# Rotary embedding of 67 MB: casts in the DMA queue against fp32 transfers with casts on ScalarE

## The chip, the cores and the metric

The kernel runs on one core of a Trainium2 chip. The metric is device time in microseconds (us) for one launch. The time before is 323.0 us, the median of 10 runs, which lie between 322.83 and 323.29 us. The profile is one execution taken by the hardware profiler; its time span starts with the program's first instructions and ends with its last.

## The reference

The input x has the shape (8, 2048, 16, 64): batch, position, head, and 64 values per head, all fp32. The 64 values are 32 neighbouring pairs. Each pair is turned by an angle that depends on the position and on the pair's number, given as tables of cosines and sines of the shape (2048, 32):

```python
x1 = x_pairs[..., 0]
x2 = x_pairs[..., 1]
out1 = x1 * cos - x2 * sin
out2 = x1 * sin + x2 * cos
out = np.stack([out1, out2], axis=-1).reshape(batch, seq_len, num_heads, head_dim)
```

x has 67.1 MB and so has the output; the two tables have 0.26 MB each. Each value of x is used for two products, so there is little arithmetic for each byte moved.

## The kernel before

A tile is 512 positions of one batch: 128 partitions, each with 4 consecutive positions (K = 4) of 16 heads of 64 values, which is 4,096 values per partition. In memory a tile is one contiguous block of 2.1 MB, 16 KiB for each partition. There are 4 groups of positions (the loop over g) and 8 batches (the loop over b inside it), together 32 tiles.

The kernel computes in bf16. The load of a tile (L73) is issued by GpSimd and converts from fp32 to bf16 on the way; the store (L86) is issued by GpSimd too and converts back. No engine does a cast of x. Both use one software DMA queue, in the order in which GpSimd issues them.

Ahead of the loops SP issues eight small loads that bring the tables, group by group, into cos_sb and sin_sb (L50, L51). For each group ScalarE expands them (build_tables, L53 to L64): for each of the 4 positions, one copy writes the cosine twice for each pair and once for every head (L61), and two write the sine and the negated sine in turn (L62, L63). The results c_tab and s_tab have 4,096 values per partition, as large as a tile of x. This makes 48 ScalarE instructions.

For each tile VectorE runs three operations. The first multiplies x by the sine table into qt (L78), the second x by the cosine table into pt (L79), and the third adds to pt the values of qt with the two of each pair exchanged (L84). The exchange costs no instruction: it is an access pattern that starts at the second value and steps back by one.

There are 5 buffers for x, 4 for qt, 4 for pt, and 3 for each expanded table. A buffer's next user waits until the last reader of it is done. The order of instructions on an engine is not written out by hand: the framework's scheduler orders them, and it lets VectorE work on the operations of two neighbouring tiles in turn. GpSimd's queue holds loads and stores; a store waits there for its addition, and a load for a free x buffer.

Of the kernel before, what the change touches and what calls it, by code (L numbers as in the profile page):

```python
# [2 lines left out]

# [4 lines left out]


@with_exitstack  # L10
def kernel(
    ctx: ExitStack,
    tc: tile.TileContext,
    x: bass.AP,
    cos: bass.AP,
    sin: bass.AP,
    out: bass.AP,
):
    nc = tc.nc
    fp32 = mybir.dt.float32  # L20
    bf16 = mybir.dt.bfloat16
    mult = mybir.AluOpType.mult
    add = mybir.AluOpType.add

    B, S, H, D = x.shape
    P = 128
    K = 4
    G = S // (P * K)
    D2 = D // 2
    HD = H * D  # L30
    W = K * HD
    ntiles = B * G

    TAIL_SPLIT = 0

    x_t = x.rearrange("b (g p k) h d -> (b g) p (k h d)", p=P, k=K)
    out_t = out.rearrange("b (g p k) h d -> (b g) p (k h d)", p=P, k=K)
    cos_g = cos.rearrange("(g p k) c -> g p (k c)", p=P, k=K)
    sin_g = sin.rearrange("(g p k) c -> g p (k c)", p=P, k=K)

    consts = ctx.enter_context(tc.tile_pool(name="consts", bufs=1))
    tabpool = ctx.enter_context(tc.tile_pool(name="tabpool", bufs=3))
    xpool = ctx.enter_context(tc.tile_pool(name="xpool", bufs=5))
    qpool = ctx.enter_context(tc.tile_pool(name="qpool", bufs=4))
    opool = ctx.enter_context(tc.tile_pool(name="opool", bufs=4))

    cos_sb = consts.tile([P, G, K, D2], fp32)
    sin_sb = consts.tile([P, G, K, D2], fp32)
    for g in range(G):
        nc.sync.dma_start(out=cos_sb[:, g], in_=cos_g[g])  # L50
        nc.sync.dma_start(out=sin_sb[:, g], in_=sin_g[g])  # L51

    def build_tables(g):  # L53
        c_tab = tabpool.tile([P, W], bf16, name="c_tab")
        s_tab = tabpool.tile([P, W], bf16, name="s_tab")
        c_dst = c_tab.rearrange("p (k h i j) -> p k h i j", k=K, h=H, i=D2, j=2)
        s_dst = s_tab.rearrange("p (k h i j) -> p k h i j", k=K, h=H, i=D2, j=2)
        for k in range(K):
            c_src = cos_sb[:, g, k : k + 1, :].to_broadcast([P, H, D2, 2])
            s_src = sin_sb[:, g, k : k + 1, :].to_broadcast([P, H, D2])  # L60
            nc.scalar.copy(out=c_dst[:, k], in_=c_src)  # L61
            nc.scalar.copy(out=s_dst[:, k, :, :, 0], in_=s_src)  # L62
            nc.scalar.mul(out=s_dst[:, k, :, :, 1], in_=s_src, mul=-1.0)  # L63
        return c_tab, s_tab  # L64

    tile_idx = 0
    for g in range(G):
        c_tab, s_tab = build_tables(g)
        for b in range(B):
            i = b * G + g  # L70

            xt = xpool.tile([P, W], bf16)
            nc.gpsimd.dma_start(out=xt, in_=x_t[i])  # L73

            qt = qpool.tile([P, W], bf16)
            pt = opool.tile([P, W], bf16)

            nc.vector.tensor_tensor(out=qt, in0=xt, in1=s_tab, op=mult)  # L78
            nc.vector.tensor_tensor(out=pt, in0=xt, in1=c_tab, op=mult)  # L79
            q_swap = dataclasses.replace(  # L80
                qt, offset=qt.offset + 1, ap=[qt.ap[0], [2, W // 2], [-1, 2]]
            )
            pt3 = pt.rearrange("p (a j) -> p a j", a=W // 2, j=2)
            nc.vector.tensor_tensor(out=pt3, in0=pt3, in1=q_swap, op=add)  # L84

            nc.gpsimd.dma_start(out=out_t[i], in_=pt)  # L86
            tile_idx += 1


# [1 line left out]
_INS = ['x', 'cos', 'sin']  # L91
_OUTS = [((8, 2048, 16, 64), 'float32')]


# [23 lines left out]
```

## Time and profile before

| What | Value |
|---|---|
| Median of 10 runs | 323.0 us |
| The profiled execution | 322.89 us |
| Its span | 321.1 us |
| VectorE busy | 213.2 us (66%), 96 operations |
| ScalarE busy | 36.8 us (11%), 48 table instructions and one table load |
| GpSimd busy | 34.5 us (11%), 64 DMA issues and 4 memsets |
| Read from and written to HBM | 67.63 MB and 67.11 MB, 420 GB/s over the span |
| Median time from issue to landing | load of x 22.7 us, store 12.6 us |

The profile divides the span into 40 equal slices of 8.03 us. A digit is the busy share of an engine in a slice, in tenths; the DMA row is the mean busy share of the core's 16 DMA engines, and GB/s is what they moved, counted on the side that is written. A row of a group of instructions gives the line, the engine, the operation, the output and the inputs with their sizes, then the count, the total busy time in us and the mean duration of one in ns, and after the second bar the idle time of the engine just ahead of these instructions and what ended most of it. A DMA share above 1 in a stretch comes from packets that overlap on one DMA engine.

### The profile page before, as it was taken

To read this page: it belongs to the slowest core of one execution; us is meant where nothing else is said; L and a number is where in the kernel's file an instruction comes from. 1 tells how busy PE (TensorE), PEld (TensorE's weight loads), DVE (VectorE), ACT (ScalarE), POOL (GpSimd) and SP (SyncE) were. 2 spreads that over 40 slices of the span, in tenths; PEclk is the share of its full clock that TensorE was granted. 3 is DMA by queue.
4 is the path that set the end of the run, shared out by engine and by line. 5 is a ranking of instruction groups with operands and counts; after the bars stand their busy time and mean duration, and the time that the engine had idled before them with its cause. 6 is when DMAs were issued, how large, how long until landed. Compare 5 with 4: busy or idle time off the path is not lost.

```text
span 321.1 us, 304 instructions
## 1 busy us (share of the span) xinstructions
DVE 213.2 (66%) x96; ACT 36.8 (11%) x49; POOL 34.5 (11%) x68
## 2 busy tenths in 40 slices
DVE  0799887601999900999910999920899920899930
ACT  8698100000820000000000000000000000000000
POOL 3010100400010030010030001030001030001000
DMA  7999999999999999999999999999999999999994
GB/s 138 217 218 216 346 329 431 429 433 244 214 215 398 431 437 251 216 213 385 436 431 266 214 214 376 431 431 281 215 216 359 431 433 294 215 214 346 435 435 176
DMA packets 10370, 101.21 MB, mean 315 GB/s; under 512 B 1152, under 2 KB 2176, under 8 KB 2176
## 3 DMA queue, kind: packets, MB, share of 16 engines
q0 software_dynamic: 9216, 100.67, 101.6%
q1 hardware_dynamic: 1152, 0.52, 1.1%
q14 instruction: 2, 0.02, 0.0%
HBM read 67.63 MB, written 67.11 MB: 420 GB/s over the span
## 4 chain that ended last, share of the span: by engine, by line
DVE 42%; DMA 35%; issue 15%; POOL 3%; POOLq 0%; DVEq 0%; PEldq 0%
DMA xt<-in_x_dram 28%; DVE pt L84 17%; DVE qt L78 13%; DVE pt L79 13%; DMA out_dram<-pt 7%; POOL xt L73 2%; POOL out_dram L86 1%; POOLq L113 0%; POOLq L86 0%; DVEq L78 0%; PEldq L113 0%
## 5 line engine op out<-in xcount | busy, mean ns | idle before, releaser
L78 DVE TENSOR_TENSOR qt<-xt,s_tab 128x4096 bf16<-128x4096 bf16 x32 | 73.2, 2289 | 79.9 <-DMA xt<-in_x_dram 79.8
L79 DVE TENSOR_TENSOR pt<-xt,c_tab 128x4096 bf16<-128x4096 bf16 x32 | 73.2, 2288 | 14.3 <-ACT c_tab L61 10.1
L84 DVE TENSOR_TENSOR pt<-pt,qt 128x4096 bf16<-128x4096 bf16 x32 | 73.2, 2288 | 0.2
L86 POOL DMA_DIRECT2D out_dram<-pt x32 | 17.1, 536 | 260.3 <-DVE pt L84 260.3
L73 POOL DMA_DIRECT2D xt<-in_x_dram x32 | 17.2, 559 | 13.3 <-DVE qt L78 10.9
L62 ACT CAST s_tab<-sin_sb 128x512 bf16<-128x512 f32 x16 | 12.3, 766 | 52.3 <-DVE qt L78 48.1
L61 ACT CAST c_tab<-cos_sb 128x1024 bf16<-128x1024 f32 x16 | 16.2, 1028 | 0.5 <-DMA cos_sb<-in_cos_dram 0.5
L63 ACT ACTIVATE s_tab<-sin_sb 128x512 bf16<-128x512 f32 x16 | 12.3, 768 | 0.0
L61 ACT ACT_TABLE_LOAD x1 | 1.3, 1283 | 0.7 <-PEq L102 0.7
L102 POOL MEMSET const-float32-0.0<- 128x1 f32 x1 | 0.1, 99 | 0.2 <-issue 0.2
L102 POOL MEMSET const-bfloat16-1.0<- 128x1 bf16 x1 | 0.1, 102 | 0.0
L102 POOL MEMSET const-uint8-127<- 128x1 uint8 x1 | 0.1, 100 | 0.0
L102 POOL MEMSET const-float32-1.0<- 128x1 f32 x1 | 0.1, 99 | 0.0
## 6 DMA issues: line engine op xcount, KB each, us to landing
out_dram<-pt POOLq DMA_DIRECT2D x32, 2048.0 KB, 12.6
xt<-in_x_dram POOLq DMA_DIRECT2D x32, 1024.0 KB, 22.7
cos_sb<-in_cos_dram SPq DMA_DIRECT2D x4, 64.0 KB, 13.1
sin_sb<-in_sin_dram SPq DMA_DIRECT2D x4, 64.0 KB, 17.7
```

Source lines behind the costliest of these rows:

```text
L61: nc.scalar.copy(out=c_dst[:, k], in_=c_src)
L62: nc.scalar.copy(out=s_dst[:, k, :, :, 0], in_=s_src)
L63: nc.scalar.mul(out=s_dst[:, k, :, :, 1], in_=s_src, mul=-1.0)
L73: nc.gpsimd.dma_start(out=xt, in_=x_t[i])
L78: nc.vector.tensor_tensor(out=qt, in0=xt, in1=s_tab, op=mult)
L79: nc.vector.tensor_tensor(out=pt, in0=xt, in1=c_tab, op=mult)
L84: nc.vector.tensor_tensor(out=pt3, in0=pt3, in1=q_swap, op=add)
L86: nc.gpsimd.dma_start(out=out_t[i], in_=pt)
L102: nc = _bacc.Bacc("TRN2", target_bir_lowering=False, num_devices=1)
```

## The change

The load of x becomes a plain fp32 transfer, issued by SP. The store becomes a plain fp32 transfer, issued by ScalarE on the Activation queue. The casts are ScalarE copies: `halve` turns the fp32 tile xt into the bf16 tile xh, and `store` turns the bf16 result pt into the fp32 tile ot ahead of its DMA.

The tables are no longer expanded over the heads. Three VectorE operations build s_tab and c_tab once for all positions, with 64 values for each position, the sine negated for the second value of each pair. The multiplications read each row of 64 values again for each of the 16 heads, with a step of 0 in the access pattern.

The order of the work is written out by hand. SP issues the load of the first tile, then one transfer for all cosines and one for all sines, and then four more loads of x. After that ScalarE's order is: cast of tile i+1, output cast of tile i, store of tile i. The load of tile i+5 is issued on SP, and needs the x buffer that the cast of tile i frees. There are 5 fp32 buffers for xt, 2 each for xh, qt and pt, and 4 fp32 buffers for ot. The order of the loops over groups and batches is as before, and so are the three VectorE operations for each tile.

```diff
-            xt = xpool.tile([P, W], bf16)
-            nc.gpsimd.dma_start(out=xt, in_=x_t[i])
+    def load(i):
+        g, b = groups[i]
+        xt = xpool.tile([P, W], fp32, name="xt")
+        nc.sync.dma_start(out=xt, in_=x_t[b, g])
+        loaded[i] = xt
 
+    def halve(i):
+        xh = hpool.tile([P, W], bf16, name="xh")
+        nc.scalar.copy(out=xh, in_=loaded.pop(i))
+        halved[i] = xh
 
+    def rotate(i):
+        g, _ = groups[i]
+        xh = halved.pop(i)
+        qt = hpool.tile([P, W], bf16, name="qt")
+        pt = hpool.tile([P, W], bf16, name="pt")
...
+        def tab(a):
+            return dataclasses.replace(
+                a,
+                offset=a.offset + g * K * D,
+                ap=[a.ap[0], [D, K], [0, H], [1, D]],
+            )
 
-            nc.vector.tensor_tensor(out=qt, in0=xt, in1=s_tab, op=mult)
-            nc.vector.tensor_tensor(out=pt, in0=xt, in1=c_tab, op=mult)
+        nc.vector.tensor_tensor(out=rows(qt), in0=rows(xh), in1=tab(s_tab), op=mult)
+        nc.vector.tensor_tensor(out=rows(pt), in0=rows(xh), in1=tab(c_tab), op=mult)
...
-            nc.gpsimd.dma_start(out=out_t[i], in_=pt)
+    def store(i):
+        g, b = groups[i]
+        ot = opool.tile([P, W], fp32, name="ot")
+        nc.scalar.copy(out=ot, in_=rotated.pop(i))
+        nc.scalar.dma_start(out=out_t[b, g], in_=ot)
+
+    with tc.manual_schedule():
+        load(0)
+        nc.sync.dma_start(out=cos_sb, in_=cos_t)
+        nc.sync.dma_start(out=sin_sb, in_=sin_t)
+        for i in range(1, NX):
+            load(i)
+        s2 = s_tab.rearrange("p g k (i j) -> p (g k i) j", j=2)
+        sin_flat = sin_sb.rearrange("p g c -> p (g c)")
+        nc.vector.tensor_copy(out=s2[:, :, 0], in_=sin_flat)
+        nc.vector.tensor_scalar_mul(s2[:, :, 1], sin_flat, -1.0)
+        nc.vector.tensor_copy(
+            out=c_tab.rearrange("p g k (i j) -> p (g k i) j", j=2),
+            in_=cos_sb.rearrange("p g c -> p (g c)").to_broadcast([P, G * K * D2, 2]),
+        )
+        halve(0)
+        for i in range(n):
+            if i + 1 < n:
+                halve(i + 1)
+            rotate(i)
+            store(i)
+            if i + NX < n:
+                load(i + NX)
```

More of the change, by code (lines that the diff above doesn't have):

```diff
@@ L29 @@
     D2 = D // 2
[L30 to L39, printed above, removed]
+    W = K * H * D
+    NX = 5
+    x_t = x.rearrange("b (g p k) h d -> b g p (k h d)", p=P, k=K)
+    out_t = out.rearrange("b (g p k) h d -> b g p (k h d)", p=P, k=K)
@@ L41 @@
+    cos_t = cos.rearrange("(g p k) c -> p g (k c)", p=P, k=K)
+    sin_t = sin.rearrange("(g p k) c -> p g (k c)", p=P, k=K)
     consts = ctx.enter_context(tc.tile_pool(name="consts", bufs=1))
-    tabpool = ctx.enter_context(tc.tile_pool(name="tabpool", bufs=3))
-    xpool = ctx.enter_context(tc.tile_pool(name="xpool", bufs=5))
-    qpool = ctx.enter_context(tc.tile_pool(name="qpool", bufs=4))
+    xpool = ctx.enter_context(tc.tile_pool(name="xpool", bufs=NX))
+    hpool = ctx.enter_context(tc.tile_pool(name="hpool", bufs=2))
@@ L45 @@
     opool = ctx.enter_context(tc.tile_pool(name="opool", bufs=4))
[L47 to L70, printed above, removed]
-            xt = xpool.tile([P, W], bf16)
-            nc.gpsimd.dma_start(out=xt, in_=x_t[i])
[L75 to L81, printed above, removed]
-            )
[L83 to L87, printed above, removed]
+    cos_sb = consts.tile([P, G, K * D2], fp32)
@@ new lines @@
+    sin_sb = consts.tile([P, G, K * D2], fp32)
+    c_tab = consts.tile([P, G, K, D], bf16)
+    s_tab = consts.tile([P, G, K, D], bf16)
+    groups = [(g, b) for g in range(G) for b in range(B)]
+    n = len(groups)
+    loaded, halved, rotated = {}, {}, {}
+    def load(i):
[7 more added lines that the diff above has]
+        halved[i] = xh
@@ new lines, in rotate, with rows @@
+    def rotate(i):
[3 more added lines that the diff above has]
+        pt = hpool.tile([P, W], bf16, name="pt")
+        def rows(a):
+            return a.rearrange("p (k h e) -> p k h e", k=K, h=H, e=D)
+        def tab(a):
[3 more added lines that the diff above has]
+                ap=[a.ap[0], [D, K], [0, H], [1, D]],
+            )
+        nc.vector.tensor_tensor(out=rows(qt), in0=rows(xh), in1=tab(s_tab), op=mult)
+        nc.vector.tensor_tensor(out=rows(pt), in0=rows(xh), in1=tab(c_tab), op=mult)
+        q_swap = dataclasses.replace(
+            qt, offset=qt.offset + 1, ap=[qt.ap[0], [2, W // 2], [-1, 2]]
+        )
+        pt3 = pt.rearrange("p (a j) -> p a j", j=2)
+        nc.vector.tensor_tensor(out=pt3, in0=pt3, in1=q_swap, op=add)
+        rotated[i] = pt
```

## The prediction

> **What bounds the kernel now.** I began with the page's slices and queue totals.
>
> ```profile
> span 321.1 us, 304 instructions
> DVE  0799887601999900999910999920899920899930
> DMA  7999999999999999999999999999999999999994
> ...
> q0 software_dynamic: 9216, 100.67, 101.6%
> q1 hardware_dynamic: 1152, 0.52, 1.1%
> ```
>
> The DMA row is full from the second slice to the last but one; VectorE has empty stretches in every round. So the transfers decide. The next view takes stretches of the span: length, busy time of VectorE, ScalarE and GpSimd, clock, DMA share, and GB/s.
>
> ```profile
> 0.00:1.50 1.50, 0.00 (x0) 0.76 (x1) 0.44 (x5) 1.00 0.00 0
> 1.50:2.50 1.00, 0.00 (x0) 0.53 (x1) 1.00 (x3) 1.00 0.36 105
> 2.50:316.50 314.00, 213.19 (x96) 35.55 (x48) 33.05 (x62) 1.00 1.05 322
> 316.50:317.70 1.20, 0.00 (x0) 0.00 (x0) 0.00 (x0) 1.00 0.10 27
> 317.70:321.10 3.40, 0.00 (x0) 0.00 (x0) 0.00 (x0) 1.00 0.00 0
> ...
> 160.00:208.00 48.00, 32.40 (x15) 0.00 (x0) 5.34 (x10) 1.00 1.05 322
> ```
>
> Start 2.5 us, saturated transfer 314.0 us, last receipt 1.2 us, closing 3.4 us: 321.1 us. The profiled execution took 322.89 us, so 1.8 us lie outside the span; the median of the runs is 0.1 us higher.
>
> The GB/s count a load by what lands, in bf16. Two more stretches show what the engines really carry:
>
> ```profile
> 272.00:288.00 16.00, 13.73 (x7) 0.00 (x0) 0.54 (x1) 1.00 1.03 216
> 296.00:316.00 20.00, 11.57 (x6) 0.00 (x0) 1.60 (x3) 1.00 1.06 433
> ```
>
> The first is loads alone: 216 landing is 432 read as fp32. The second is stores alone: 433 written as fp32. Either way the fp32 side limits, at about 432 GB/s. One tile of a steady round lands 1.049 MB and writes 2.097 MB, 3.146 MB at 322 GB/s: **9.77 us a tile**. 32 tiles are 312.6 us, which leaves 1.4 us of the 314.0 for the tables. (Their queue share, 1.1% of 321.1 us, is 3.5 us, overlapped with other packets.)
>
> Compute lies below this:
>
> ```profile
> L78 DVE TENSOR_TENSOR qt<-xt,s_tab 128x4096 bf16<-128x4096 bf16 x32 | 73.2, 2289 | 79.9 <-DMA xt<-in_x_dram 79.8
> L79 DVE TENSOR_TENSOR pt<-xt,c_tab 128x4096 bf16<-128x4096 bf16 x32 | 73.2, 2288 | 14.3 <-ACT c_tab L61 10.1
> L84 DVE TENSOR_TENSOR pt<-pt,qt 128x4096 bf16<-128x4096 bf16 x32 | 73.2, 2288 | 0.2
> L86 POOL DMA_DIRECT2D out_dram<-pt x32 | 17.1, 536 | 260.3 <-DVE pt L84 260.3
> L61 ACT CAST c_tab<-cos_sb 128x1024 bf16<-128x1024 f32 x16 | 16.2, 1028 | 0.5 <-DMA cos_sb<-in_cos_dram 0.5
> ```
>
> VectorE steps at 2.20 us an operation in the chain of waits, so a tile costs 2.29 + 2 x 2.20 = 6.7 us. Its 79.8 us of waiting for x are the mark of a transfer-bound kernel. At the end one more view, instructions in order of time, matters:
>
> ```profile
> 303.38 0.53 POOL L86 DMA_DIRECT2D out_dram<-pt  x1 [6.07 <-DVE pt L84]
> 305.32 2.29 DVE L84 TENSOR_TENSOR pt<-pt,qt 128x4096 bf16<-128x4096 bf16 x1
> 307.90 0.53 POOL L86 DMA_DIRECT2D out_dram<-pt  x1 [4.00 <-DVE pt L84]
> ```
>
> The last store is issued at 307.9 us, and the transfers stay full until 316.5: stores had piled up behind the last loads, so the last tile's compute is covered whole.
>
> [...] L84, with its swapped pairs, shows only that an odd pattern can run as fast as the plain L78.
>
> **The change part by part.**
>
> *Bytes.* A load still reads 2.097 MB of fp32, a store still writes it; only the other side of each grows to fp32. The limiting side is unchanged: 32 x 9.77 = 312.6 us at the old rate[...]. I take +0.5 us, 313.1. Tables: again 1,024 packets of 512 bytes; 1.4 us, at most 3.5.
>
> *Start.* The first large load leaves GpSimd at 1.26 us now; SP issued its first transfer at 0.74. I take full transfer from 1.9 instead of 2.5: -0.6 us (0 to -0.8).
>
> *Tables.* Removed: 48 ScalarE instructions, 16.2 + 12.3 + 12.3 = 40.8 us, under full transfers: worth 0. Added: three VectorE operations on 512, 512 and 1,024 elements[...]. On SP's queue two table issues (0.42 us each, as SP's row of issues in time shows) stand between load 0 and load 1. Their data come behind load 0's 4.9 us, so the tables are in at about 9.2 us (11.3 at the worst), built by 12 to 14, and the first multiply starts 2 to 4 us later than today's 10.1. Cover: loads 1 to 4 keep the transfers full until about 28 us, and the first store's data follow at about 25.5. Cost 0; without that cover, the 2 to 4 us.
>
> *Casts.* Added: 64 ScalarE copies of 4,096 elements. [...] Per tile 2 x 3.6 + 0.5 for the store's issue (GpSimd's took 0.536, SP's 0.42) + about 0.2 of handover = 7.9 us, under 9.77: no bound, 1.9 us of slack. Each microsecond beyond the slack would cost 32.
>
> *Multiplies with compact tables.* 6.7 us a tile as today, covered[...].
>
> *Issues moved off GpSimd.* 64 x 0.54 us go from an engine that limited nothing: 0. SP's load i+5 waits for cast i to free its x buffer; only later loads stand behind it.
>
> *The new order on ScalarE.* This is the cost that I expect. Cast i+1 stands in front of the output cast and the store of tile i, so each store waits for the next tile's load. In the middle other loads fill the transfers. At the end none are left. Say the last load lands at T. Cast 3.6, rotation 6.7, output cast 3.6, issue and first data about 1.3, handovers 0.4: store 31 moves data from T + 15.6. Store 30 must follow cast 31 and its own cast: data from T + 8.5, for 4.9 us. Store 29 began near T - 1.3 and has 4.2 to 4.9 us left. So the transfers have 9.1 to 9.8 us of work in 15.6: **idle 5.8 to 6.5 us**. If the two queues share evenly, stores run at half speed beside loads, one more store is left over at T (4.9 us), and the idle time falls to 0.9 to 1.6. If loads run ahead and finish early, ScalarE's 7.9 us a tile against 4.9 us a store leaves up to 10. I take 4.0.
>
> *Sum.* Start 1.9 + payload 313.1 + tables 1.4 + idle 4.0 + receipt 1.2 + closing 3.4 = 325.0 us of span against 321.1; with 1.8 outside, **326.8 us**, a forecast of +3.8 us on the median (0.1 allowed either way).
>
> **Rivals.**
>
> *Two: the tail is covered and the start's gain remains* (faster or equal). For it: one leftover store at T is enough, since its 4.9 us fill most of the gap[...]. Idle 0 to 1: 1.9 + 312.6 + 1.4 + 0.5 + 4.6 + 1.8 = 322.8; with a rate of 434, which some stretches show, payload is 309.2 and the time 319.4. It decides against the forecast where idle is under about 1 us at the old rate, or the rate is over 1% better. Against it: evenness has to hold up to the last tile.
>
> [...]
>
> *Four: loads and stores mixed on every DMA engine run below 428.* [...] At 420: payload 319.5, time 333[...]. Today's rounds change from loads to stores without a dip, but as one queue; that does not exclude it.
>
> That the casts would not move to ScalarE, I exclude: a plain copy between types is what L61 is today.
>
> **How the numbers follow.** Forecast 0.53 (own range 323.3 to 330), rival two 0.24, three 0.03, four 0.20. What one can tell from no change here is 0.2%, or 0.65 us: 322.35 to 323.65. Rival two gives 0.17 faster, 0.06 same, 0.01 slower; the forecast's low end 0.05 same. So 0.17, 0.11, 0.72. The range 320 to 335 leaves out rival three, half of four and a little of two: about 0.16.
>
> **What would show it.** Right: x rows fp32 on SP, two ScalarE rows of x32 near 3.6 us; multiplies still 2.29; GB/s near 430 now in all slices, since both sides are fp32; a dip only in the last slices; the chain of waits ending cast, three VectorE operations, cast, store. Wrong if the middle slices lie under 425 (rival four)[...], or the last stores run without a gap (two). Periodic dips would say that ScalarE's order costs something in the middle too, which I priced at nothing.

## The result and the profile after

The changed kernel takes 319.9 us (median of 8 runs, 319.54 to 320.27) against 322.98 us for the kernel before in the same comparison: a ratio of 0.9904, 95% interval 0.9895 to 0.9912. It is 3.1 us faster. The forecast was 3.8 us slower: the time moved the other way.

The page of the changed kernel, slices and queues:

```profile
span 318.0 us, 335 instructions
DVE  0698999866668766678666687666786666876650
ACT  1599999688766688666786666876667866768750
DMA  7999999999999999999999999999999999999997
...
q1 hardware_dynamic: 5664, 67.64, 50.2%
q10 hardware_dynamic: 4608, 67.11, 49.3%
```

The DMA row has no dip, not even at the end: where the kernel before closed with a 4 the changed one closes with a 7. The queues of SP (q1) and of ScalarE (q10) have equal shares of the engines over the whole span, as they move equal bytes. They share evenly in the middle too: in each 40 us from 60 to 260 us the packets of the trace give either queue 212 to 218 GB/s. The groups of the same page:

```profile
L60 ACT CAST xh<-xt 128x4096 bf16<-128x4096 f32 x32 | 115.4, 3606 | 76.5 <-DMA xt<-in_x_dram 74.8
L79 DVE TENSOR_TENSOR qt<-xh,s_tab 128x4096 bf16<-128x4096 bf16 x32 | 73.4, 2292 | 76.7 <-ACT xh L60 76.7
L91 ACT CAST ot<-pt 128x4096 f32<-128x4096 bf16 x32 | 115.3, 3602 | 3.6 <-DVE pt L85 3.6
L80 DVE TENSOR_TENSOR pt<-xh,c_tab 128x4096 bf16<-128x4096 bf16 x32 | 73.1, 2285 | 0.0
...
xt<-in_x_dram SPq DMA_DIRECT2D x32, 2048.0 KB, 38.8
out_dram<-ot ACTq DMA_DIRECT2D x32, 2048.0 KB, 25.3
```

The casts take 3.6 us, the multiplies on the short table rows 2.292 and 2.285 us, against 2.289 and 2.288 before. ScalarE now waits for x (74.8 us), as VectorE did. A store lands 25.3 us after its issue, which is 2.6 tiles of 9.7 us. That last number is the one that the prediction lacked. The stretches of the changed kernel, cut at the cast of the last tile (295.9 us), at the first data of the last store (about 311), at the end of the busy engines (315.8) and where SP goes on (317.3):

```profile
1.50:4.00 2.50, 0.00 (x0) 0.51 (x1) 0.00 (x0) 1.00 0.90 229
4.00:295.90 291.90, 210.90 (x96) 217.14 (x62) 0.00 (x0) 1.00 1.01 431
295.90:311.00 15.10, 7.51 (x4) 10.70 (x3) 0.00 (x0) 1.00 1.00 428
311.00:315.80 4.80, 0.00 (x0) 0.00 (x0) 0.00 (x0) 1.00 0.98 416
315.80:317.30 1.50, 0.00 (x0) 0.00 (x0) 0.00 (x0) 1.00 0.03 11
```

The 15.1 us in which the last tile is computed run at 428 GB/s. The engines were busy from about 1.5 to 315.8 us, 314.3 us, and for 314.0 in the kernel before. The gain is therefore not in the rate of the transfers. Compare the ends. The stores of the changed kernel (count, then shortest, median and longest issue in ns, then first and last start; below that the times to landing, the shortest of which is the last store's):

```profile
L92 ACTq DMA_DIRECT2D out_dram<-ot x32: 338/338/379, 22.5 to 310.0; - x32
DMA to landing us min/median/max: 7.1/25.3/25.8
```

The last landing is at 310.0 + 7.1 = 317.1 us, and the span ends at 318.0, 0.9 us later. In the kernel before the last landing is at 317.7 us and the span ends at 321.1, 3.4 us later. Of the 3.1 us, **2.6 are behind the last landing** and 0.5 ahead of it. What fills the time behind it is a line which the prediction does not use, the closing instructions of the kernel before (numbers as above):

```profile
L113 SPq EVENT_SEMAPHORE  x11: 17/28/28, 317.7 to 321.1; - x11
L113 POOLq DRAIN  x3: 45/101/12464, 307.9 to 320.9; - x3
```

GpSimd's drain, the long one of its three DRAIN instructions, starts at 307.9 us, behind the last issue, and lasts 12.464 us: until 320.4. SP has seen the last landing at 317.7 and then waits, 2.2 us in one piece, until the drain is over; 0.8 us after the drain the span ends. In the changed kernel the lines of the closing read

```profile
L141 POOLq DRAIN  x3: 34/41/75, 0.7 to 317.7; - x3
L141 SPq DRAIN  x3: 7/7/7, 317.3 to 317.6; - x3
```

so nothing there is long: SP goes on at 317.3 us, and the span ends 0.7 us later.

### The profile page after: what moved, and what is told of

Same layout as the page of the kernel before. It is cut to its first block, busy times and chain, and to the rows that moved or that the text cites. A ratio compares the mean times of both kernels' runs of the same rounds, so it can differ in the third digit from the quotient of the medians.

```text
span 318.0 us, 335 instructions
## 1 busy us (share of the span) xinstructions
DVE 218.4 (69%) x99; ACT 229.1 (72%) x65; POOL 0.2 (0%) x4
## 4 chain that ended last, share of the span: by engine, by line
DMA 78%; ACT 13%; DVE 4%; issue 2%; ACTq 1%; SPq 0%
DMA xt<-in_x_dram 78%; ACT ot L91 7%; ACT xh L60 7%; DVE pt L85 1%; DVE qt L79 1%; DVE pt L80 1%; ACTq L92 1%; SPq L55 0%
## 5 line engine op out<-in xcount | busy, mean ns | idle before, releaser
L60 ACT CAST xh<-xt 128x4096 bf16<-128x4096 f32 x32 | 115.4, 3606 | 76.5 <-DMA xt<-in_x_dram 74.8
L79 DVE TENSOR_TENSOR qt<-xh,s_tab 128x4096 bf16<-128x4096 bf16 x32 | 73.4, 2292 | 76.7 <-ACT xh L60 76.7
L91 ACT CAST ot<-pt 128x4096 f32<-128x4096 bf16 x32 | 115.3, 3602 | 3.6 <-DVE pt L85 3.6
L80 DVE TENSOR_TENSOR pt<-xh,c_tab 128x4096 bf16<-128x4096 bf16 x32 | 73.1, 2285 | 0.0
L104 DVE CAST c_tab<-cos_sb 128x1024 bf16<-128x1024 f32 x1 | 0.7, 684 | 0.0
## 6 DMA issues: line engine op xcount, KB each, us to landing
xt<-in_x_dram SPq DMA_DIRECT2D x32, 2048.0 KB, 38.8
out_dram<-ot ACTq DMA_DIRECT2D x32, 2048.0 KB, 25.3
```

Source lines behind the costliest of these rows:

```text
L60: nc.scalar.copy(out=xh, in_=loaded.pop(i))
L79: nc.vector.tensor_tensor(out=rows(qt), in0=rows(xh), in1=tab(s_tab), op=mult)
L80: nc.vector.tensor_tensor(out=rows(pt), in0=rows(xh), in1=tab(c_tab), op=mult)
L91: nc.scalar.copy(out=ot, in_=rotated.pop(i))
L104: nc.vector.tensor_copy(out=c_tab.rearrange("p g k (i j) -> p (g k i) j", j=2), in_=cos_sb.rearrange("p g c -> p (g c)").to_broadcast([P, ...
```

## The experiments

Two questions: what makes the drain last 2.7 us beyond the last landing, and why the tail that I had priced at 4.0 us of idle transfers has none.

### One software transfer, at the end or at the start

`pool_last`:

```diff
-        nc.scalar.dma_start(out=out_t[b, g], in_=ot)
+        eng = nc.gpsimd if i == n - 1 else nc.scalar
+        eng.dma_start(out=out_t[b, g], in_=ot)
```

> The changed kernel with one difference: the store of the last tile is issued by GpSimd on the software queue, still plain fp32. Theory A (the gain sits mainly behind the last byte: in the kernel before, GpSimd's closing drain lasts until 320.4 us, 2.7 us after the last landing at 317.7, and the changed kernel has no such drain): the time comes back by 2.5 to 3 us, to 322.4 to 322.9 us, with the last packet at the same place as in the changed kernel, 316.3 us, and GpSimd's drain ending some 2.7 us after the landing. Theory B (the gain comes from faster or earlier transfers on the SP and Activation queues): unchanged, 319.9 us within 0.5.

Measured: 320.46 us (320.08 to 320.90). Theory A missed: only some 0.5 us came back. The drain of this run:

```profile
L142 POOLq DRAIN  x3: 39/93/6991, 310.5 to 318.0; - x3
```

It ends at 310.5 + 7.0 = 317.5 us, within 0.1 us of the landing (310.6 + 6.9), and the 0.3 us between the spans (318.3 and 318.0) lie ahead of the landing. One software transfer at the end is not what costs.

`pool_first`:

```diff
-        nc.sync.dma_start(out=xt, in_=x_t[b, g])
+        eng = nc.gpsimd if i == 0 else nc.sync
+        eng.dma_start(out=xt, in_=x_t[b, g])
```

> The changed kernel with the load of tile 0 alone issued by GpSimd. Theory A, if the drain waits for the software queue's latest transfer: that transfer is long over at the end, so the closing stays short and the time is 319.9 us, or up to 1 us more for the later start of the first bytes. Theory A, if any use of the software queue costs the drain: 322.5 us. Theory B: the start is what counts, so about 1 us more, 320.9 us.

Measured: 320.23 us (320.08 to 320.32), 0.3 us more, as the first of its three expectations has it. The drain is over early:

```profile
L142 POOLq DRAIN  x3: 34/92/12192, 1.2 to 318.1; - x3
```

It ends at 1.2 + 12.2 = 13.4 us, 0.1 us after the landing of tile 0 at 13.3. The run showed something else too. Tile 0 landed later, the first store was issued at 27.5 us instead of 22.5, and from then on the stores landed 35.0 us after issue instead of 25.3, until the loads ended. The output cast even waited 11.0 us in all for its buffers. The store backlog (stores issued and not yet landed) that was made in the opening stayed in this run: near its end one tile's cast still followed another after 9.74 us (281.65 to 291.39), and one store another after 9.78 us (279.65 to 289.43).

### The software queue's share of the work

`half_in` (fp32 loads and the input cast as in the change; the store with the cast in GpSimd's queue):

```diff
-        ot = opool.tile([P, W], fp32, name="ot")
-        nc.scalar.copy(out=ot, in_=rotated.pop(i))
-        nc.scalar.dma_start(out=out_t[b, g], in_=ot)
+        nc.gpsimd.dma_start(out=out_t[b, g], in_=rotated.pop(i))
```

with pt in the pool of 4 buffers.

> Only the input side of the change: fp32 loads on SP with a ScalarE cast, but the store is GpSimd's, bf16 in and fp32 out, 32 of them on the software queue up to the end. pool_last showed that one software store at the end closes in 0.3 us more, not 2.7. Theory A2 (the closing grows with the number of transfers that the software queue has carried, or with those still queued when GpSimd is done issuing): GpSimd's drain ends 1.3 to 2.7 us after the last landing. Theory C (the 2.7 us of the kernel before come from something other than GpSimd's queue): the closing is 0.6 us. The time: A2 321 to 323 us, C 319.5 to 320.5, if the tail is covered as in the changed kernel.

`half_out` (the load with the cast in GpSimd's queue; output cast and store as in the change):

```diff
-        xt = xpool.tile([P, W], fp32, name="xt")
-        nc.sync.dma_start(out=xt, in_=x_t[b, g])
+        xt = xpool.tile([P, W], bf16, name="xt")
+        nc.gpsimd.dma_start(out=xt, in_=x_t[b, g])
...
-        nc.scalar.copy(out=xh, in_=loaded.pop(i))
-        halved[i] = xh
+        halved[i] = loaded.pop(i)
```

> Only the output side: the load is GpSimd's with a cast in the queue (32 software transfers, the last issued some 60 us before the end), the output is cast on ScalarE and stored as fp32 on the Activation queue. A2 by number: a closing of 1.3 us more than the changed kernel's; A2 by what is still queued at the end: no more than 0.3 us. Theory C: none. Loads alone land 216 GB/s and read 432; the first loads start at about 2.6 us as in the kernel before, so 319.5 to 321.5 us in every case, and the length of the drain tells.

`pool_all` (the changed kernel with all loads and stores on GpSimd, plain fp32):

```diff
-        nc.sync.dma_start(out=xt, in_=x_t[b, g])
+        nc.gpsimd.dma_start(out=xt, in_=x_t[b, g])
...
-        nc.scalar.dma_start(out=out_t[b, g], in_=ot)
+        nc.gpsimd.dma_start(out=out_t[b, g], in_=ot)
```

> The changed kernel with all 64 transfers of x and the output on GpSimd's software queue, still plain fp32, the ScalarE casts kept. It separates the queue from the cast. A2: the closing is the kernel before's 3.4 us from landing to end, so at least 2.7 us come back: 322.5 us or more. If the closing is 0.7 us here, the casts in the queue made it long. The single queue also orders loads and stores as issued: each load stands behind the store of five tiles earlier; the transfers stay full if the five loads ahead suffice, which I expect.

Measured: half_in 325.87 us (above both expectations), half_out 322.48 (321.54 to 324.88, above its expectation; against the kernel before a ratio of 0.9991, interval 0.9973 to 1.0008: no difference), pool_all 325.42. The drains, in this order:

```profile
L139 POOLq DRAIN  x3: 45/101/7886, 314.8 to 323.6; - x3
```

```profile
L139 POOLq DRAIN  x3: 39/93/45541, 254.2 to 319.5; - x3
```

```profile
L141 POOLq DRAIN  x3: 45/82/12522, 310.4 to 323.3; - x3
```

In half_in SP sees the last landing at 321.4 us and the drain ends at 322.7: 1.3 us later in the trace, half of 2.7. In half_out it is over at about 299.8 us, 20 us before the span ends, and costs nothing at the end. In pool_all, where no queue casts, it ends at 322.9, 2.7 us after the landing that SP sees at about 320.2, as in the kernel before. So casts are not the reason, and the drains that came early (here and in pool_first) were hidden.

The remaining microseconds are other things. The profiled execution of half_out is its fastest, 321.54 us, with a span 1.8 us longer than the changed kernel's: its last landing is at about 318.5 us instead of 317.1, and 1.3 us instead of 0.9 lie behind it. What makes its other executions slower is not known. half_in has a gap: its last x cast starts at about 304 us, not at 295.9, less of a backlog is left at that point (8.8 us at 423 GB/s, 3.7 MB, against 15.1 us at 428, 6.5 MB), and the transfers run dry:

```profile
304.00:312.80 8.80, 5.03 (x3) 3.60 (x1) 0.00 (x0) 1.00 1.04 423
312.80:315.60 2.80, 1.76 (x1) 0.00 (x0) 0.53 (x1) 1.00 0.01 0
315.60:320.60 5.00, 0.00 (x0) 0.00 (x0) 0.00 (x0) 1.00 1.02 419
```

Gap 2.8 and closing 1.5 more (2.4 us, from 321.4 to 323.8, against 0.9) make 4.3 of the 5.8 us between the spans; where the rest lies was not shown. The late cast waited for its load: in the whole run the x casts wait 190.3 us for loads, against 74.8 in the changed kernel, and a load lands 45.2 us after its issue, against 38.8. What makes the loads late was not tested. In pool_all the transfers fall to 88 GB/s at 316.8 us, with a mean DMA share of 0.21, and go on so for 2.8 us:

```profile
300.00:316.80 16.80, 6.41 (x3) 6.71 (x2) 1.06 (x2) 1.00 0.97 413
316.80:319.60 2.80, 0.00 (x0) 0.00 (x0) 0.00 (x0) 1.00 0.21 88
```

### Number or bytes

`pool_count` (pool_last, and 62 transfers of 2 KB at the start):

```diff
+        for m in range(62):
+            nc.gpsimd.dma_start(out=scrap[:, m], in_=cos[0:16, :])
```

> The run with the last store on GpSimd, and beside it 62 small software transfers (16 rows of 128 bytes of the cosine table into a scratch tile that nothing reads) issued by GpSimd at the start: 63 software transfers instead of 1, with almost the same bytes. The drain after the last landing has been 2.7 us with 64 software transfers in the kernel before, 2.5 with 64 fp32 ones, 1.3 with 32, none with 1. Theory A2 by number: 2.4 to 2.8 us between the landing and the end of GpSimd's drain; the small transfers add up to 3.5 us of transfer, so the time is 322.7 to 326 us, and the trace decides. By bytes or packets of the software queue: no more than 0.3 us, 320.5 to 324 us.

`split_before` (the kernel before):

```diff
-            nc.gpsimd.dma_start(out=out_t[i], in_=pt)
+            nc.gpsimd.dma_start(out=out_t[i, :, : W // 2], in_=pt[:, : W // 2])
+            nc.gpsimd.dma_start(out=out_t[i, :, W // 2 :], in_=pt[:, W // 2 :])
```

> The kernel before with each store issued as two, one for each half of the columns: 96 software transfers instead of 64, the same bytes. A2 by number: 96 times 42 ns is 4.0 us of drain after the last landing instead of 2.7: the time rises by 1.3 us, to 324.3 us, if the transfers themselves stay as they are (the packets of stores are halved to 8 KiB). If the drain goes by bytes: 2.7 us still, 323.0 us.

Measured: pool_count 324.25 us, split_before 325.59. The drains:

```profile
L145 POOLq DRAIN  x3: 46/107/9356, 312.2 to 322.1; - x3
```

```profile
L114 POOLq DRAIN  x3: 45/101/13536, 309.5 to 323.5; - x3
```

pool_count: the last store is issued at 312.2 us and lands 6.7 us later, at 318.9; the drain ends at 321.6, 2.6 us after it, with 2.2 MB moved by this queue and not 134. Its 62 small transfers were over by about 117 us (the last issued at 99.0, none longer than 17.5 to landing), so they count though none was waiting at the end. split_before: landing 319.1, drain until 323.0, 4.0 us in the trace. The drain behind the last software landing went by the **number of software transfers**: 1, 32, 63, 64 and 96 gave about 0.1, 1.3, 2.6, 2.7 and 4.0 us (both runs with 1 and both with 64 agree), some 41 ns each. What GpSimd does in that time the traces do not show. The 1.8 us by which pool_count's landing is later than the changed kernel's (318.9 against 317.1) lie in the transfers, which end at about 318.0 us against 315.8. split_before is slower than expected by another 1.3 us, since its last landing is 1.4 us later than the unsplit kernel's (319.1 against 317.7).

### The backlog of stores

`ot2` (2 buffers for the fp32 output), and `ot3` likewise with 3:

```diff
-    opool = ctx.enter_context(tc.tile_pool(name="opool", bufs=4))
+    opool = ctx.enter_context(tc.tile_pool(name="opool", bufs=2))
```

> The changed kernel with 2 buffers for the fp32 output instead of 4. Stores can then wait at most two deep; the changed kernel has 2.6 tiles of them in flight (25.3 us from issue to landing against 9.7 us a tile). Theory A (that backlog is what fills the 15.6 us from the last load's landing to the last store's first byte): the transfers run dry near the end for 4 to 6 us, the time is 323.5 to 326 us, and the dip lies in the last two slices alone. Theory B (the tail would be filled in any case): 319.9 us within 0.5.

> The changed kernel with 3 buffers for the fp32 output. With 2 the stores land 15.7 us after issue, the tail has a gap and the time is 324.9 us; with 4 they land after 25.3 us, with no gap. The changed kernel's last store is issued at 310.0 us, its data follow at about 311, and the transfers end at 315.8, 4.9 us later: the gap is just closed. Theory A: three stores in flight are at most 25 us at 9.7 us each, less what the waiting output cast takes; a gap of 0 to 2 us, 320 to 322 us. Theory B, which ot2 spoke against: 319.9 us.

Measured: ot2 324.90 us (324.85 to 325.24), ot3 319.79 (319.69 to 320.00). With two buffers the stores land after 15.7 us, and the tail of the last tile is no longer covered; the stretches of ot2:

```profile
260.00:300.00 40.00, 28.26 (x14) 30.79 (x9) 0.00 (x0) 1.00 1.01 431
300.00:306.00 6.00, 4.23 (x3) 5.59 (x3) 0.00 (x0) 1.00 0.81 344
306.00:312.00 6.00, 5.96 (x3) 3.18 (x1) 0.00 (x0) 1.00 0.59 249
312.00:318.00 6.00, 0.52 (x1) 3.60 (x1) 0.00 (x0) 1.00 0.65 276
```

At 344, 249 and 276 of 431 GB/s over 6 us each, 1.2 + 2.5 + 2.2 = 5.9 us are lost; the spans differ by 5.3 us, 323.3 to 318.0, and the last store lands 0.8 us sooner after its issue here (6.3 us, 7.1 in the changed kernel). The middle keeps its 431. So without room for the backlog the tail was not covered. How much of the loss is the backlog alone this run does not tell, for the same edit makes ScalarE wait for output buffers (58.1 us in 28 waits): the last load has landed by 297.3 us (issued at 258.3, and no load took over 39.0), but its cast comes only at 302.1, behind an output cast that waited 0.9. In the changed kernel the covering itself can be seen: the trace has nothing but stores, the rest of 27 to 30, in the 15.1 us after the last load, at 428 GB/s. ot3 has 25.0 us from issue to landing, all the backlog that there is, no such wait, and loses nothing; there I expected up to 2 us too much.

`nx3`:

```diff
-    NX = 5
+    NX = 3
```

> The changed kernel with 3 buffers for the fp32 input instead of 5. Theory A says more exactly that the backlog of stores is made in the opening, by tiles that land before the loads and the stores share the engines, and is kept since both queues then run at equal rates: with fewer tiles ahead there is less of it, the stores land 15 to 20 us after issue instead of 25.3, and the tail shows a gap of 1 to 5 us: 321 to 325 us. Theory B: 319.9 us within 0.5. If three buffers starve the loads in the middle as well, dips show in all slices and this run tells neither.

Measured: 319.87 us, and the stores again land after 25.3 us. My account of how the backlog is made was wrong in its detail. Load 3 needs cast 0 alone, which ended at 12.0 us in the changed kernel, before loads 0 to 2 had all been moved (the data of load 2 end at 19.3 us there); so three buffers let the loads run ahead of the first store, as five do; that store was issued at 22.6 us, against 22.5. More loads in flight than that gained nothing here.

### The short packets of the tables

`tab2k`: positions given to the partitions in runs of 16.

```diff
-    x_t = x.rearrange("b (g p k) h d -> b g p (k h d)", p=P, k=K)
+    x_t = x.rearrange("b (p g k) h d -> b g p (k h d)", p=P, k=K)
-    cos_t = cos.rearrange("(g p k) c -> p g (k c)", p=P, k=K)
+    cos_t = cos.rearrange("(p g k) c -> p g (k c)", p=P, k=K)
```

and the output and the sine table alike.

> The changed kernel with the 2,048 positions given to the partitions in one run of 16 each, so that a table row of a partition is one piece of 2 KiB instead of four of 512 bytes, 256 packets for the tables instead of 1,024; x rows stay 16 KiB, at a distance of 64 KiB. The SP queue's share of the engines exceeds the Activation queue's by 0.9% of 318.0 us, 2.8 us, for 0.52 MB that would take 1.2 us at 431 GB/s. Theory D (short packets cost): up to 1.6 us less, 318.3 to 319.5 us. Theory E (the packets overlap others and cost nothing): 319.9 us within 0.4. If the 64 KiB distance slows the large transfers: above 321 us, with GB/s under 425 in the middle.

Measured: 319.84 us (319.83 to 319.87). Theory E: 768 fewer short packets are worth nothing that shows, and a distance of 64 KiB between the rows of a tile did no harm (431 GB/s in the middle).

None of these runs is faster than the changed kernel by more than 0.1 us, which is less than its own scatter. With 134.7 MB at 431 GB/s, 312.6 us, in a span of 318.0, little is left but the start and the closing.

## Why the prediction was wrong

**The bound, the transfers, the casts and the multiplies: right.** A tile takes 4.194 MB / 431 GB/s = 9.73 us against 9.77. The two queues together reached 431 GB/s; I had added 0.5 us for a slightly lower rate; at 431 that term is -1.2 us instead. The casts measure 3.606 and 3.602 us against 3.6, which was my estimate: the kernel before has no copy of this size. The issue of a store on ScalarE took 0.34 against 0.5. The repeated table rows ran at 2.292 and 2.285 us, as the full rows did: rival three, a slower VectorE on these rows, is out; no trace had shown such a thing. Rival four, a mix below 428, is out by the middle stretches, with 431 GB/s; its 420 was an estimate.

**The closing, 3.4 us carried over unchanged: most of the gain.** The sum took "receipt 1.2 + closing 3.4" from the kernel before without asking what fills the 3.4 us. For 2.7 us it was GpSimd's drain, and all 64 issues with which it grows were being removed; the 0 for the issues moved off GpSimd is the first step that failed. Measured: closing 0.9, which is 2.5 us less than the 3.4 of the sum.

**The idle tail, 4.0 us: wrong, and the larger error of the forecast.** The timing of the step was right: the last store's data were to start 15.6 us after the last load's landing, and did after 15.1. What the transfers had to do in the meantime was not. I counted stores 29 and 30, 9.1 to 9.8 us of work, and one store more under even sharing, which still left 0.9 to 1.6 us idle; the 4.0 lay between the cases. Measured: 15.1 us at 428 GB/s, 6.5 MB, 3.1 stores: store 28 and a rest of store 27 were still to be moved as well. Even sharing, which the kernel before could not show, was true (212 to 218 GB/s for each queue), and the opening had left 2.6 tiles of stores in flight. The gap was closed with almost nothing to spare: the last store's data follow those of store 30 at once, and begin 0.9 us after their issue; in ot2, where nothing stood ahead of them, it was about 0.8 (issue at 316.2 us, the 2.1 MB of the store from 317 to 322).

**The start.** The engines were busy from about 1.5 us instead of 1.9. SP's two table issues between the loads left no gap, as said (from 8 to 9 us, behind load 0, the DMA share is 1.15 to 1.20 at 347 to 366 GB/s), and tab2k gained nothing from fewer table packets; the three table operations took 1.6 us, and the first multiply came at 12.0 us, at the early end of the 12 to 14, which were my estimate.

The forecast's span of 325.0 less 4.0 of idle time and 2.5 of closing is 318.5. The start is 0.4 us earlier, the busy stretch 0.2 us shorter and the receipt 0.1 us longer than in the sum, which gives the measured 318.0. Rival two named the right outcome, a covered tail, but it too kept the closing of 3.4 us: had the drain stayed, the gain would have been 0.5 us. Its second figure, 319.4 us, lies near the measured 319.9 by luck, since it takes the gain from a rate of 434 GB/s.

## What to carry to other kernels

Look up what stands between the last landing and the end of the span before carrying it over, above all when a change moves transfers from one issuing engine to another: here that piece was 2.6 of 3.1 us, and no busy share showed it. When loads and stores share the DMA engines from two queues, ask how many stores are in flight when the last load lands; here they held 15.1 us of transfers, as much as the last tile's compute chain took, and the chain was free; the number of output buffers must allow that many (three did, and two did not).

## What was not expected of the hardware

- GpSimd's drain behind the last software landing grew with the number of software transfers of the whole kernel, about 41 ns each (1, 32, 63, 64, 96 transfers: 0.1, 1.3, 2.6, 2.7, 4.0 us), whatever their bytes and whether they cast.
- With all 64 fp32 transfers on the software queue, the transfers ended with 2.8 us at 88 GB/s and a mean DMA share of 0.21, after 413 GB/s. With stores on the Activation queue, in the changed kernel, this was not seen: 451 GB/s from 315.2 to 315.6 us were followed by 41 in the next 0.4 us.
- The issue of a store on the Activation queue took 0.34 us on ScalarE.
- With fp32 loads on SP's queue and casting stores on the software queue (half_in), the last x cast waited for its load until 304.1 us, against 295.9 in the changed kernel; the cause is open.
